# Strassen products in a hybrid decoder layer: seven half-size products for eight, hidden activations in DRAM, and a recurrence on doubling blocks

## The chip, the cores and the metric

The kernel runs on one core of a Trainium2 chip. A core has a matrix engine (TensorE, "PE" in the profile, with "PEld" for its weight loads), VectorE ("DVE"), ScalarE ("ACT"), GpSimd ("POOL") and SyncE ("SP"), which here issues all DMA transfers. Each runs its own list of instructions in order, and semaphores join them. The metric is the device time of one execution in microseconds.

## The reference

One decoder layer on 1024 tokens of width 1024, in float32, and a final norm.

```python
x = x + 0.5 * swiglu(rms(x), ffn1_w1, ffn1_w3, ffn1_w2)         # 1024 -> 2816 -> 1024
proj = rms(x) @ w_in                # q, f, i, og (8 heads x 128 each), pool 512, gates A and B
f = lb + (1 - lb) * sigmoid(f_r); k = 1 - f; q = silu(q_r); v = i_r
S_t = diag(f_t) S_{t-1} + k_t outer v_t;  o_t = S_t^T q_t       # per head, 128 x 128 state
y_a = (rms_per_head(o) * silu(og)) @ w_branch_a
y_b = (group_map(trailing_means(pool) - pool) * scale) @ w_branch_b
x = x + (sigmoid(ga) * y_a + sigmoid(gb) * y_b) @ w_out
x = x + 0.5 * swiglu(rms(x), ffn2_w1, ffn2_w3, ffn2_w2)
x = x + sigmoid(rms(x) @ ple_w_gate) * rms(p @ ple_w_proj)
return rms(x)
```

## The kernel before, in words

Every large product runs as three passes of float32r matmuls. `split` (L104 to L106) cuts a float32 operand into a high part (a ScalarE cast, L105) and a low part (a VectorE subtraction, L106); `mm3` (L119 to L122) sums high x high, high x low and low x high in PSUM. A full matmul has 128 x 128 stationary values and 512 moving columns.

There are two forms of product. `up` (L124) holds 128 weight columns stationary and moves 512 tokens: the result is feature-major, [128 features, 512 tokens], one PSUM bank, 8 chunks of the inner dimension, 24 matmuls. The token-major products (`down_tiles` L216, `down_half` L706 hold 128 tokens stationary and move 512 columns of weights. The residual `x` is token-major in SBUF as 16 tiles of [128, 512]; `norm_t` (L175) scales its rows, transposes them on TensorE against an identity (L187) and splits them into feature-major tiles.

`ffn` (L202) takes 22 chunks of 128 hidden features in groups of two. Of each chunk `up_chunk` makes w1 and w3 products for both halves of the tokens, the sigmoid gate and the split; `down_tiles` adds the chunk pair's part of the downward product to `x` at once (L224). The downward products run one group behind, and the hidden activations never leave SBUF.

In the mixing stage, `head_in` makes q, f, k and silu(og) of one head and half the tokens with `up`; v is made token-major for two heads at a time with 256 moving columns. `hgrn` (L417) runs the recurrence of one head over half the tokens in four chunks of 128: the decay between two tokens is a product of f's over blocks, in three steps of four neighbouring blocks (h = 1, 4, 16; score matmuls at L498 with 192 columns, or with ones at L505 and L506 where h = 1), and a last step between blocks of 64 tokens (L518). Masked copies (L510) put a step's scores in place, `grow` (L443) widens the blocks. Then follow k transposed (L531), the states of the chunks (L535, L544), the outputs (L553, L555), a norm per head and a transpose (L570). The heads' loop runs two inputs ahead. The gates, branch B, branch A, `w_out`, the second FFN and the embedding gate follow; the embedding's own product was made at the start and waits in DRAM.

The order of instructions on each engine is not written out. A planner goes through the program with a model of costs: program order gives the priority, an instruction may go ahead of an earlier one that isn't ready, and a tile's slot must be free before it is written. Tiles of one tag share a fixed number of slots: 54 units of [128, 512] ("u"), 12 split weight tiles of [128, 1024] ("w"), 4 raw weight tiles and some smaller sets. All DMA transfers go through SP's queue in planned order.

Of the kernel before, what the change touches and what calls it, by code (L numbers as in the profile page):

```python
# [15 lines left out]
AX = mybir.AxisListType  # L16
# [6 lines left out]
FC = 22  # L23
HEADS = 8
# [3 lines left out]
STEPS = (1, 4, 16)  # L28

N_RAW = 4  # L30
WARM = 11
N_W = 12
# units [128, 512]: main, temporaries, per chain of the recurrence (two tags each), states
BANKS = {"mm": 2, "aux0": 1, "aux1": 1, "sc0": 1, "sc1": 1}
UNITS = {"u": 54, "t": 4, "h0": 2, "h1": 2, "st": 3, "qx0": 1, "qx1": 1}
# [3 lines left out]
def hybrid_block(ctx: ExitStack, tc: tile.TileContext, a: dict, out: bass.AP):  # L39
    """One decoder layer and the final norm.  # L40

    Products run as three float32r passes: each float32 operand is split exactly into
    two parts of 12 bits (hi = round(x), lo = x - hi), and hi*hi + hi*lo + lo*hi is summed
    in PSUM.  The residual is held token-major; activations that feed a product with
    stationary weights are held feature-major, as hi and lo units [128, 512 tokens].
    """
    nc = tc.nc
    const = ctx.enter_context(tc.tile_pool(name="const", bufs=1))
    big = ctx.enter_context(tc.tile_pool(name="big", bufs=1))
# [9 lines left out]
    def unit(s, dt=F32, tag="u"):  # L59
        return big.tile([P, HALF], dt, tag=tag, name=name(s), bufs=UNITS[tag])  # L60

    def raw(s, shape=(P, 1024)):
        return big.tile(list(shape), F32, tag="raw", name=name(s), bufs=N_RAW)

    def wtile(s):
        return big.tile([P, 1024], F32R, tag="w", name=name(s), bufs=N_W)

    def bank(s="mm"):
        return psum.tile([P, HALF], F32, tag=s, name=name(s), bufs=BANKS[s])

# [4 lines left out]
    ident = small("ident", [P, P])  # L75
    make_identity(nc, ident)
    ones = small("ones", [P, P], F32R)
    nc.vector.tensor_scalar(ones, ident, 0.0, 1.0, ALU.mult, ALU.add)
# [3 lines left out]
    for h in STEPS:  # L82
        # columns of a step (see hgrn), rows s: 1 where s lies in the block of h tokens
        # that the column's target block takes as its source
        n = 32 // h
        m = small(f"mask{h}", [P, 192], BF16)
        nc.gpsimd.memset(m, 1.0)
        for at, blocks, first, move in ((0, 3, 0, 1), (96, 2, 0, 0), (160, 1, 1, 0)):
            mv = m[:, at : at + 32 * blocks].rearrange("p (a j h) -> p a j h", a=n, h=h)
            for sign, base in ((1, -first * h), (-1, first * h + h - 1)):  # L90
                nc.gpsimd.affine_select(
                    out=mv, in_=mv,
                    pattern=[[-sign * 4 * h, n], [-sign * move * h, blocks], [0, h]],
                    compare_op=ALU.is_ge, fill=0.0, base=base, channel_multiplier=sign,
                )
        masks[h] = m
# [11 lines left out]
    def load(ap, s):  # L108
        r = raw(s)
        nc.sync.dma_start(out=r, in_=ap)  # L110
        return r

    def weight(ap, s):
        r = load(ap, s)
        hi, lo = wtile(s + "h"), wtile(s + "l")
        split(r, hi, lo)
        return hi, lo

    def mm3(ps, ah, al, bh, bl, first, last):  # L119
        nc.tensor.matmul(ps, ah, bh, start=first, stop=False)  # L120
        nc.tensor.matmul(ps, ah, bl, start=False, stop=False)  # L121
        nc.tensor.matmul(ps, al, bh, start=False, stop=last)  # L122

    def up(w, act, half, off=0):  # L124
        """[128 columns, 512 tokens] of act @ w; w = (hi, lo) tiles whose column blocks of 128
        are the stationary operands."""
        ps = bank()
        n = len(act)
        for k in range(n):
            ah, al = act[k][half]  # L130
            c = slice(off + k * P, off + (k + 1) * P)
            mm3(ps, w[0][:, c], w[1][:, c], ah, al, k == 0, k == n - 1)
        return ps

    def token(act, k, t):
        ah, al = act[k][t // 4]
        c = slice((t % 4) * P, (t % 4 + 1) * P)
        return ah[:, c], al[:, c]

    def pair(s, tags=("u", "u")):  # L140
        return unit(s + "h", F32R, tags[0]), unit(s + "l", F32R, tags[1])

# [1 line left out]
    def rstd_of(rs, ss, n):  # L144
        nc.vector.tensor_tensor(rs, ss[:, 0:1], ss[:, 1:2], ALU.add)
        nc.vector.tensor_scalar(rs, rs, 1.0 / n, EPS, ALU.mult, ALU.add)
        nc.gpsimd.tensor_tensor(rs, rs, mhalf[:, 0:1], ALU.pow)  # L147
# [3 lines left out]
    def stat():  # L151
        stat_n[0] += 1
        ss = const.tile([P, 2], F32, tag="ss", name=name("ss"), bufs=4)
        rs = const.tile([P, 1], F32, tag="rs", name=name("rs"), bufs=4)
        return ss, rs

    def gain_rows(ap, s):
        g = raw(s)
        nc.sync.dma_start(out=g, in_=ap.partition_broadcast(P))
        return g  # L160

    def normed_row(x, g, t):
        """rms-normed token tile: two units [128 tokens, 512]."""
        ss, rs = stat()
        xn = [unit("xn"), unit("xn")]
        for d in range(2):
            nc.scalar.activation(xn[d], x[t][d], AF.Square, accum_out=ss[:, d : d + 1])
        rstd_of(rs, ss, D)
        for d in range(2):
            nc.vector.scalar_tensor_tensor(  # L170
                xn[d], x[t][d], rs[:, 0:1], g[:, d * HALF : (d + 1) * HALF], ALU.mult, ALU.mult
            )
        return xn

    def norm_t(x, g, between=None):  # L175
        """rms-normed x, feature-major and split: act[k][half] = (hi, lo).  Traces the first
        half of the tokens and returns a function that traces the second."""
        act = [[None, None] for _ in range(KC)]

        def rows(half):  # L180
            return [normed_row(x, g, 4 * half + t) for t in range(4)]

        def part(half, xn):
            for k in range(KC):
                ps = bank(("sc0", "sc1", "aux0", "aux1")[k % (2 + 2 * half)])
                for t in range(4):
                    nc.tensor.transpose(  # L187
                        ps[:, t * P : (t + 1) * P],
                        xn[t][k // 4][:, (k % 4) * P : (k % 4 + 1) * P],
                        ident,  # L190
                    )
                act[k][half] = pair("h")
                split(ps, *act[k][half])

        xn = rows(0)
        if between is not None:
            between()
        part(0, xn)
        return act, lambda: part(1, rows(1))
# [135 lines left out]
    def opening():  # L335
        for d in range(2):
            embed(0, d)
# [540 lines left out]
```

## Time and profile before

| | |
|---|---|
| timed runs | median 2550.24 us of 3 (2549.74 to 2550.61) |
| profiled execution | span 2549.6 us from first to last instruction; no other time of it is recorded, so the span stands 0.6 us under the median of the runs |
| PE busy | 2521.0 us, 11923 matmuls |
| weight loads | 2094.3 us |
| VectorE | 1227.1 us, 2132 instructions |
| ScalarE | 624.2 us, 1155 instructions |
| GpSimd | 57.7 us, 155 instructions |
| DMA | 154.19 MB, 60 GB/s over the span |
| granted TensorE clock | 0.999 |

Busy time adds up the durations of instructions. Matmuls are pipelined: one is listed with 0.39 us, but the next starts after about 0.23, so time per matmul is read from start times. A float32 matmul (not float32r) is listed as two records. "Idle before" is time in which an engine had nothing to run, with what ended it. A row of a group gives line, engine, operation, output and inputs by name, shapes and count, then busy time, mean nanoseconds of one, and the idle time before.

### The profile page before, as it was taken

The page shows a single profiled execution, that of the slowest core. Times are in us where ns is not written, and L with a number is a line of the kernel's source. Part 1 is how long each engine was busy: PE and PEld are TensorE (multiplying, and loading weights), DVE is VectorE, ACT ScalarE, POOL GpSimd, SP SyncE. Part 2 cuts the span into 40 slices and gives each one's busy share as a digit, 9 for nine tenths or more (in the row PEclk, how much of TensorE's full clock was granted, in tenths as well). Part 3 has the DMA queues.
Part 4 walks back from the last instruction along what each step waited for, and adds up shares of the span by engine and source line. Part 5 has one row for each costly group of instructions (what it writes and reads, how often), then busy time and mean ns, then how long its engine had stood idle before and what let it go on. Part 6 is the DMA issues. An engine that isn't in the chain of part 4 may idle for free.

```text
span 2549.6 us, 28969 instructions
## 1 busy us (share of the span) xinstructions
PE 2521.0 (99%) x11923; PEld 2094.3 (82%) x11923; DVE 1227.1 (48%) x2132; ACT 624.2 (24%) x1155; POOL 57.7 (2%) x155
## 2 busy tenths in 40 slices
PE   8999999999999999999999999999999999999998
PEld 6888888888888888888888888888888888888877
DVE  5344433333456758585852206344344334434475
ACT  6211111111124323333323113123111111111253
POOL 2000000000000000000000000000000000000010
PEclk9999999999999999999999999999999999999999
DMA  7111111111121111111111104321111111111132
GB/s 248 42 50 50 50 50 50 50 50 50 58 94 56 58 38 46 41 43 46 34 59 45 47 25 140 108 67 42 50 50 50 50 50 50 48 43 43 46 119 84
DMA packets 54372, 154.19 MB, mean 60 GB/s; under 512 B 6112, under 2 KB 6624, under 8 KB 54240
## 3 DMA queue, kind: packets, MB, share of 16 engines
q1 hardware_dynamic: 54240, 152.34, 18.4%
q8 instruction: 93, 1.52, 0.3%
q14 instruction: 39, 0.32, 0.0%
HBM read 135.54 MB, written 16.78 MB: 60 GB/s over the span
## 4 chain that ended last, share of the span: by engine, by line
PE 91%; DVE 5%; issue 1%; ACT 1%; DMA 1%; POOL 0%; SPq 0%; POOLq 0%; ACTq 0%; DVEq 0%
PE mm L121 22%; PE mm L122 22%; PE mm L120 22%; PE aux L120 6%; PE aux L121 6%; PE aux L122 6%; PE sc L498 2%; DVE score L510 1%; PE sc L187 1%; DVE xn L170 1%; PE aux L535 1%; PE aux L553 1%; PE aux L555 0%; PE aux L518 0%; POOL rs L147 0%
## 5 line engine op out<-in xcount | busy, mean ns | idle before, releaser
L224 DVE SCALAR_TENSOR_TENSOR x<-aux,x 128x512 f32<-128x512 f32 x352 | 241.2, 690 | 191.8 <-PE aux L122 190.3
L120 PE MATMUL aux<-w2h,gh 128*128 128x512 f32 x704 | 276.4, 393 | 1.6 <-DVE x L224 1.5
L120 PE MATMUL mm<-hh,w1h 128*128 128x512 f32 x704 | 274.9, 390 | 1.0 <-ACT hh L105 1.0
L121 PE MATMUL mm<-hl,w1h 128*128 128x512 f32 x704 | 274.6, 390 | 0.0
L122 PE MATMUL mm<-hh,w1l 128*128 128x512 f32 x704 | 274.5, 390 | 0.0
L121 PE MATMUL aux<-w2l,gh 128*128 128x512 f32 x704 | 274.3, 390 | 0.0
L122 PE MATMUL aux<-w2h,gl 128*128 128x512 f32 x704 | 274.0, 389 | 0.0
L120 PE MATMUL mm<-hh,w3h 128*128 128x512 f32 x704 | 274.0, 389 | 0.0
L122 PE MATMUL mm<-hh,w3l 128*128 128x512 f32 x704 | 273.9, 389 | 0.0
L121 PE MATMUL mm<-hl,w3h 128*128 128x512 f32 x704 | 273.9, 389 | 0.0
L211 DVE TENSOR_TENSOR sg<-sg,mm 128x512 f32<-128x512 f32 x88 | 60.5, 688 | 284.5 <-PE mm L122 284.5
L120 PEld LDWEIGHTS aux<-w2h,gh 128*128 128x128 f32 x704 | 132.1, 188 | 35.1 <-DVE x L224 8.3
L120 PEld LDWEIGHTS mm<-hh,w1h 128*128 128x128 f32 x704 | 132.1, 188 | 28.5 <-ACT hh L105 1.5
L122 PEld LDWEIGHTS aux<-w2h,gl 128*128 128x128 f32 x704 | 132.2, 188 | 27.8
L120 PEld LDWEIGHTS mm<-hh,w3h 128*128 128x128 f32 x704 | 132.2, 188 | 27.6 <-DVE x L746 0.2
L121 PEld LDWEIGHTS mm<-hl,w3h 128*128 128x128 f32 x704 | 132.2, 188 | 27.4
L122 PEld LDWEIGHTS mm<-hh,w3l 128*128 128x128 f32 x704 | 132.1, 188 | 27.4
L121 PEld LDWEIGHTS mm<-hl,w1h 128*128 128x128 f32 x704 | 132.2, 188 | 27.1
L122 PEld LDWEIGHTS mm<-hh,w1l 128*128 128x128 f32 x704 | 132.2, 188 | 27.0
L121 PEld LDWEIGHTS aux<-w2l,gh 128*128 128x128 f32 x704 | 132.2, 188 | 26.5
L120 PE MATMUL mm<-hh,wih 128*128 128x512 f32 x384 | 153.8, 401 | 0.0
L122 PE MATMUL mm<-hh,wil 128*128 128x512 f32 x384 | 153.5, 400 | 0.0
(234 smaller groups left out, 4286.0 us busy)
## 6 DMA issues: line engine op xcount, KB each, us to landing
w<-in_ffn_w_dram SPq DMA_DIRECT2D x132, 512.0 KB, 3.6
wi<-in_w_in_dram SPq DMA_DIRECT2D x24, 512.0 KB, 3.6
x<-in_x_dram SPq DMA_DIRECT2D x16, 256.0 KB, 7.4
e_dram<-e SPq DMA_DIRECT2D x16, 256.0 KB, 5.9
x_dram<-x SPq DMA_DIRECT2D x16, 256.0 KB, 2.0
wv<-in_w_v_dram SPq DMA_DIRECT2D x8, 512.0 KB, 3.5
o_dram<-og SPq DMA_DIRECT2D x16, 256.0 KB, 2.0
wgb<-in_w_in_dram SPq DMA_DIRECT2D x8, 512.0 KB, 3.5
```

The lines of the kernel that those rows point to most:

```text
L120: nc.tensor.matmul(ps, ah, bh, start=first, stop=False)
L121: nc.tensor.matmul(ps, ah, bl, start=False, stop=False)
L122: nc.tensor.matmul(ps, al, bh, start=False, stop=last)
L170: nc.vector.scalar_tensor_tensor(xn[d], x[t][d], rs[:, 0:1], g[:, d * HALF : (d + 1) * HALF], ALU.mult, ALU.mult)
L187: nc.tensor.transpose(ps[:, t * P : (t + 1) * P], xn[t][k // 4][:, (k % 4) * P : (k % 4 + 1) * P], ident,)
L211: nc.vector.tensor_tensor(s, s, pb, ALU.mult)
L224: nc.vector.scalar_tensor_tensor(x[t][d], ps, 0.5, x[t][d], ALU.mult, ALU.add)
L498: nc.tensor.matmul(ps[:, c, :192], kc[c], qx[:, c, :], start=True, stop=True)
L510: nc.vector.copy_predicated(s4[:, :, :, (4 - blocks) * hh :], sect(m4, lo, blocks), sect(ps, lo, blocks))
L535: nc.tensor.matmul(p_, a_, b_, start=True, stop=True)
L553: nc.tensor.matmul(p_, sc[:, c, :], vc[c], start=True, stop=s_ is None)
```

## The change

All large products but the embedding's use Strassen's scheme in Winograd's form: with each operand in four quarters, eight quarter products become seven products of sums and differences of quarters. The names are A for the weights' side (A11, A12, A22, S1 to S4) and B for the activations' side (B11, B21, B22, T1 to T3, N4); `SIDES` says which go together. The quarters are of the inner dimension (even and odd chunks of 128), of the weight columns (two chunks, such as w1 and w3 of one hidden chunk, or two column blocks of the projection) and of the tokens (two halves of 512).

- `prep` loads the two weight tiles of a pair, makes S1 to S4 with four GpSimd operations of [128, 512], and splits them: 10 tiles of the "w" tag, which has 12. `up_pair` runs seven products of 12 matmuls, and reads each result once with ScalarE or VectorE. `run_pair` leaves products 4 and 3 of a pair to run after products 1 and 2 of the next one.
- `act_first` makes B11 and B21 from the first half of the tokens after a norm; `act_second` makes the rest, with two VectorE differences from PSUM and two GpSimd differences for every two feature chunks. A full set takes 28 tiles of [128, 1024], all of tag "a".
- An FFN makes all 22 chunks first (`ffn_up`); the hidden activations and their sums (four GpSimd operations for two chunks) go to DRAM. `ffn_down` then reads them back in three groups of inner chunks (8, 8 and 6), with w2's quarters loaded and combined (six GpSimd differences of up to [128, 1024] a group, and two later), and x read again from DRAM.
- `tok` runs a token-major product: seven products, each over four blocks of 128 tokens, two lines of PSUM banks. After the fifth of the seven products (of the last group, in the downward one) the next norm's first half is begun.
- In the mixing stage v, the output gate, gates A and B, pooled and mixed values go through DRAM. v is made feature-major and transposed in `hgrn`. The loop over heads places one gate or pool pair behind each head. The recurrence takes seven levels (blocks of 1, 2, 4 to 64 tokens), each with four matmuls of 64 columns, a copy into the scores, and one multiplication that grows q's right halves and k's left halves together; before them, the diagonal comes from one product of k and q.
- Branch B's and A's activations are loaded and combined by `load_act`; `w_out` and the embedding gate combine both operands on GpSimd (`tok_sides`).
- silu is one ScalarE function instead of a sigmoid and a product. The host only moves axes (and repeats rows of w2 to fill its last group, which aren't used).

```diff
+ROOM = {"a": (1024, 28), "w": (1024, 12), "q": (1024, 4), "u": (512, 8), "h": (512, 5)}
+BANKS = {"pA": 2, "pB": 2, "pC": 1, "aux": 3}
...
+    def act_second(act, b11, b21, b12, b22):
+        t1, t3 = t_("w", "t1"), t_("w", "t3")
+        nc.vector.tensor_tensor(t1[:, L], b12, b11, ALU.subtract)
+        nc.vector.scalar_tensor_tensor(t3[:, L], b12, -1.0, b22, ALU.mult, ALU.add)
+        act["B22"].append(hilo_half(b22, "a", "x3"))
+        pool_sub(t1[:, R], b22, t1[:, L])
+        pool_sub(t3[:, R], b21, t1[:, R])
+        for t, names in ((t1, ("T1", "T2")), (t3, ("T3", "N4"))):
+            for n_, hl in zip(names, halves(hilo(t, "a", "x" + names[0]))):
+                act[n_].append(hl)
...
+        load(ra, wa)
+        load(rb, wb)
+        w = {}
+        w["A11"], w["A12"] = halves(hilo(ra, "w", "wa"), m)
+        pool_add(s[:, one], rb[:, one], rb[:, two])
+        pool_sub(s[:, two], s[:, one], ra[:, one])
+        w["S1"], w["S2"] = halves(hilo(s, "w", "ws"), m)
+        w["A22"] = hilo_half(rb[:, two], "w", "wd")
+        pool_sub(rb[:, one], ra[:, one], rb[:, one])
+        pool_sub(rb[:, two], ra[:, two], s[:, two])
+        w["S3"], w["S4"] = halves(hilo(rb, "w", "wt"), m)
...
+    SIDES = {
+        1: ("A11", "B11"), 2: ("A12", "B21"), 3: ("S4", "B22"), 4: ("A22", "N4"),
+        5: ("S1", "T1"), 6: ("S2", "T2"), 7: ("S3", "T3"),
+    }
...
+        pa, pb, pc = bank("pA"), bank("pB"), bank("pC")
+        product(1, pa, True)
+        nc.scalar.copy(c1, pa)
+        product(2, pc, True)
+        add(c1, c1, pc)
+        yield c1
+        product(6, pa, False)
+        nc.scalar.copy(c2, pa)
+        product(5, pb, True)
+        product(7, pa, False)
+        nc.scalar.copy(c3, pa)
+        add(c3, c3, pb)
+        yield c3
+        product(4, pa, False)
+        yield pa
+        product(3, pb, False)
+        add(c2, c2, pb)
+        yield c2
...
+        for i in order:
+            ls, rs = lhs(i), rhs(i)
+            line = int(i in (2, 5, 3))
+            start = i in (1, 2, 5)
+            for j in range(4):
+                if start:
+                    banks[line][j] = bank(TOK_TAGS[line][j])
+                ps = banks[line][j]
+                c = slice(j * P, (j + 1) * P)
+                for k, ((ah, al), (bh, bl)) in enumerate(zip(ls, rs)):
+                    mm3(ps, ah[:, c], al[:, c], bh, bl, start and k == 0, k == len(ls) - 1)
+                read(i, j, ps)
+            if i in between:
+                between[i]()
...
+        for hh in LEVELS:
+            n = 64 // hh
+            ps = bank("aux").rearrange("p (c x) -> p c x", c=4)
+            m = 64 if hh == 64 else P
+            for c in range(4):
+                right = qc[c].rearrange("p (a two h) -> p a two h", two=2, h=hh)[:, :, 1, :]
+                nc.tensor.matmul(ps[:m, c, :64], kc[c][:, :m], right, start=True, stop=True)
...
+            both = view(qk, hh, [[HALF - hh, 2], [2 * hh, na], [1, hh]])
+            by = view(tots[hh], 0, [[1, 2], [2, na], [0, hh]])
+            mul(both, both, by)
```

More of the change, by code (lines that the diff above doesn't have):

```diff
@@ L574, in hgrn @@
[L574 to L602 removed]
+        ps = bank("aux")
```

1191 lines of the change are left out of this document (609 added, 582 removed).

## The prediction

> **What bounds the kernel now.** I read the page's engine shares first, then its chain of waits, then busy time in stretches, then single instructions.
>
> ```profile
> span 2549.6 us, 28969 instructions
> PE 2521.0 (99%) x11923; PEld 2094.3 (82%) x11923; DVE 1227.1 (48%) x2132; ACT 624.2 (24%) x1155; POOL 57.7 (2%) x155
> PE 91%; DVE 5%; issue 1%; ACT 1%; DMA 1%; POOL 0%; SPq 0%; POOLq 0%; ACTq 0%; DVEq 0%
> ```
>
> In the table of stretches the columns are the stretch, its length, busy time and count of PE, weight loads, VectorE, ScalarE and GpSimd, the granted clock, the DMA share and GB/s.
>
> ```profile
> 100.00:700.00 600.00, 599.93 (x2643) 495.24 (x2642) 236.26 (x311) 99.39 (x130) 0.00 (x0) 1.00 0.15 49
> 740.00:1310.00 570.00, 560.94 (x3204) 480.40 (x3203) 406.90 (x950) 184.26 (x442) 17.95 (x19) 1.00 0.15 49
> 2540.00:2549.60 9.60, 1.76 (x15) 1.56 (x13) 3.59 (x9) 2.73 (x7) 0.55 (x1) 0.81 0.29 109
> ```
>
> TensorE is never without work: 28.6 us of the span are not PE, of which 8 lie at the end (2540 to 2549.6), 9 in the recurrence (740 to 1310) and the other 11 mostly at the start. In the first FFN (100 to 700) VectorE works 39% of the time and GpSimd not at all. So a matmul taken away is worth its whole pitch, as long as the other engines keep up. Pitch comes from start times, since a matmul's own 0.39 us overlaps the next:
>
> ```profile
> 863.79 0.39 PE L121 MATMUL mm<-hl,wih 128*128 128x512 f32 x1
> ...
> 866.51 0.39 PE L121 MATMUL mm<-hl,wih 128*128 128x512 f32 x1
> ...
> 900.66 0.28 PE L120 MATMUL mm<-wvh,hh 128*128 128x256 f32 x1
> ...
> 901.97 0.28 PE L122 MATMUL mm<-wvh,hl 128*128 128x256 f32 x1
> ```
>
> Twelve steps of 512 columns take 2.72 us, 0.2267 each; eleven of 256 columns take 1.31, 0.119 each.
>
> **The products.** Before, counted from the loops: each FFN 22 x 96 up and 22 x 48 down, 3168, so 6336; input projection 1152 (q, f, og), 192 (pool), 768 (gates); branch A 384, B 192, w_out 384, embedding gate 384: together 9792 of 512 columns, and 768 of 256 columns for v. That is 9792 x 0.2267 + 768 x 0.119 = 2311 us. After: 5544 in the FFNs (seven eighths), 26 pairs of projection columns at 84, 4 of branch B at 42, 4 of A at 84, 336 and 336: 8904, or 2019 us. **Minus 292 us.** The embedding product and the 256 norm transposes stay.
>
> **The recurrence on TensorE.** It runs 16 times (8 heads, 2 halves).
>
> ```profile
> 861.50 1.54 PE L498 MATMUL sc<-qx,k 128*128 128x192 f32 x8 [0.41 <-DVE score L510]
> 862.74 0.53 PE L120 MATMUL mm<-hh,wih 128*128 128x512 f32 x1
> ...
> 870.18 0.68 PE L518 MATMUL aux<-qf,k 128*64 128x64 f32 x8
> 870.79 0.50 PE L122 MATMUL mm<-hh,wil 128*128 128x512 f32 x1
> ...
> 881.38 0.34 PE L505 MATMUL sc<-qk,ones 128*128 128x384 f32 x1
> 881.56 0.34 PE L506 MATMUL sc<-qk,ones 128*128 128x384 f32 x1
> ...
> 898.02 0.60 PE L531 MATMUL aux<-ident,k 128*128 128x128 f32 x4
> 898.38 0.36 PE L120 MATMUL mm<-wvh,hh 128*128 128x256 f32 x1
> ...
> 899.30 1.16 PE L535 MATMUL aux<-v,k 128*128 128x128 f32 x8
> 900.22 0.36 PE L120 MATMUL mm<-wvh,hh 128*128 128x256 f32 x1
> ```
>
> Removed each time: two steps of four 192-column matmuls (1.24 each), four with ones at 0.18, two 512-wide ones (0.45) and the 64-token step (0.61): 4.3 us. Added: the diagonal (four 128-column ones, 0.92), four transposes of v (0.36), seven levels of four 64-column matmuls. Their price lies between 0.61 (64-wide weights) and 0.92 (128 columns) a level; most have full weights and half the columns, so I take 0.75: 5.25 in all. Net 2.2 x 16 = **plus 36 us** (20 to 55).
>
> **Can the other engines follow?**
>
> ```profile
> L106 DVE TENSOR_TENSOR w1l<-w,w1h 128x1024 fp32r<-128x1024 f32 x44 | 53.8, 1222 | 83.6 <-ACT w1h L105 83.5
> L105 ACT CAST w1h<-w 128x1024 fp32r<-128x1024 f32 x44 | 46.4, 1054 | 259.4 <-PE aux L121 172.7 <-issue 73.6 <-PE mm L121 10.8
> L224 DVE SCALAR_TENSOR_TENSOR x<-aux,x 128x512 f32<-128x512 f32 x352 | 241.2, 690 | 191.8 <-PE aux L122 190.3
> L167 ACT ACTIVATE xn<-x 128x512 f32<-128x512 f32 x64 | 39.8, 623 | 52.2 <-DVE x L224 33.4 <-DVE x L746 18.7
> L147 POOL TENSOR_TENSOR rs<-rs,mhalf 128x1 f32<-128x1 f32 x40 | 23.0, 579 | 1932.1 <-DVE rs L146 1870.5 <-DVE tot L440 48.2 <-DVE rs L145 5.3
> masks.py:199 POOL TENSOR_SCALAR_AFFINE_SELECT ident<-ident 128x128 f32<-128x128 f32 x1 | 0.3, 294 | 0.0
> L510 DVE COPY_PREDICATED score<-mask,sc 128x256 f32<-128x256 uint16 x48 | 25.6, 534 | 0.0
> L452 DVE TENSOR_TENSOR qf<-q,f 128x512 f32<-128x512 f32 x16 | 10.8, 677 | 0.0
> ```
>
> An upward pair is 84 matmuls, 19.0 us. VectorE has three 1024-wide splits and one 512-wide (4.4 us) and five 512-wide operations (3.4): 7.8 us. ScalarE has about 7. GpSimd, which did next to nothing, now makes the sums: four 512-wide ones a pair and four more every second pair. No two-input add of this size runs on it in the trace. From below an add costs VectorE's 0.68; from above, the pow row by its width is 579 ns per column, which would make the kernel impossible and is a power, not an add; nearest is the select, 294 ns for 128 columns, so 1.2 us for 512. Then GpSimd works 7 of 19 us. Twelve weight slots against ten used by a pair let the next two loads start after the second of seven products, about 13 us ahead of need; load, split and sums take about 7. So I cost the steady pairs at nothing; if that cover were gone, the load's 3.6 and the splits' 2.3 would come back at each of 70 pairs (410 us).
>
> A downward product is 48 matmuls, 10.9 us, with four 1024-wide splits and four reads: 7.7 us of VectorE. It follows, with less to spare.
>
> Beside these rows stands a rule of the Trainium skill (SBUF — State Buffer, "Who interferes with whom"): a GpSimd operation that reads SBUF and a VectorE operation with two SBUF inputs exclude each other for their whole length. No row here has both at work. By it the sum for an upward pair is unchanged, since 7 and 5 us still fit into 19; what it does at the downward groups is a rival below.
>
> **The new waits.** This decides. Before, the hidden activations stayed in SBUF and stages overlapped; now 28 wide slots are full of activation tiles during the upward products, so the next stage's tiles come from DRAM when those are let go.
>
> ```profile
> 30.00:40.00 10.00, 9.23 (x47) 7.31 (x46) 3.00 (x4) 5.82 (x10) 0.00 (x0) 1.00 1.02 363
> w<-in_ffn_w_dram SPq DMA_DIRECT2D x132, 512.0 KB, 3.6
> 20.19 0.69 PE L187 MATMUL sc<-ident,xn 128*128 128x128 f32 x2 [2.68 <-DVE xn L170]
> ...
> 20.82:23.54 2.72, 2.72 (x7) 2.14 (x7) 2.69 (x5) 0.42 (x1) 0.00 (x0) 0.50 0.61 209
> ```
>
> - **Up to down, twice.** Eight slots come free after product 2 of the last pair, seven products (19 us) before the array runs dry. In SP's queue stand eight w2 tiles, eight x tiles, then the first two chunk tiles: 18 x 0.524 = 9.4 MB. At 363 GB/s, the fastest stretch, that is 26 us; a third longer, 35. With 2.3 for the splits the wait is 9 to 18: 13 each, 26.
> - **Norm to up, twice.** Behind the last read: add 0.7, square 1.2, pow 0.6, scale 1.4, then four column groups at 4.4 us of VectorE (two PSUM reads, 2.5 widths of split), with copies and GpSimd's differences between them: about 25. Cover: products 1 and 2 (5.4), transposes (3), perhaps the next pair's first two. 12 each, 24; at the start 8.
> - **Embedding gate.** Its w tiles need slots that the FFN lets go at its end; 2.6 MB and splits, 12, and products 1, 2 wait for single-buffered splits, 4 each: 20.
> - **w_out.** 8 MB and the last y through DRAM; 15 with its own splits.
> - **Down groups.** Eight new w2 tiles at four changes of group, 4 each: 16.
> - **Branches B and A.** Half-size products (9.5 us a pair) with as many instructions, and A's last activations wait for B's: 18.
> - **Recurrence.** A level is a chain: four matmuls 0.75, masked copy 0.53, product of decays 0.68, handovers: 2.2 us, seven times 15, and some 17 around it (state, output, norm). 32 us a half, 64 a head, against some 58 us of matmuls for each odd head: 25.
>
> Sum of these, 152 (0 to 300). Nothing of it can be overtaken where tiles lack; below I keep zero because the order of instructions is planned and fills holes.
>
> **The clock.** After 2.68 us idle, matmuls ran at a granted clock of 0.50 for 2.72 us. About twelve of the waits are that long: 1.2 each, **14 us**. The Trainium skill (TensorE: Matmul & The Clock Gate, "What's actually happening") says the clock halves after an idle window of about 3.4 us; the trace halves after less. By the rule alone the gaps under its window would be free and this term about half.
>
> **The sum.** 2549.6 - 292 + 36 + 152 + 14 = 2460. The runs' median, 2550.24, is 0.6 above the span, so a timed run would read **about 2460 us**, 3.5% faster.
>
> **Rivals.**
> *The holes are filled.* For it: the planner kept the recurrence at 561 of 570 us on PE, though its chain runs over three engines. Against: a missing tile can't be planned around. Waits and clock together 50: 2549.6 - 256 + 50 = 2344 (2300 to 2390).
> *The port decides the downward groups.* Mechanism: at each group's start GpSimd makes six 1024-wide differences, 2.4 us each, 14.4, in which VectorE's splits can't run; in two products (21.7) VectorE needs 9.8 of splits and 5.5 of reads, together 29.7. Eight us late at six groups: 48, so 2508. That is the skill's exclusion named above; nothing here shows it yet.
> *Slower: the recurrence's chain ends last.* Place: one half can't begin its levels before the last has freed tiles (five narrow slots, four used by each). The stage holds 26 x 19.0 + 16 x 10 = 655 us of matmuls, 680 with my waits; the chain is 57 ahead plus 16 L. At L = 44.5 us a half it adds the 90 that make the whole gain vanish, so it decides there. At L = 50 it is 857, plus 177: 2637. For it: seven dependent levels where three wide steps stood, on a VectorE that is 71% busy in 740 to 1310. Against: ten gate and pool pairs of 19 us now lie between and behind the heads.
> That the matmuls don't fall in number would give some 2750; the seven calls leave no room for it.
>
> **How the numbers follow.** Forecast (2390 to 2540) 0.51; filled holes 0.24; port 0.07; chain 0.15; 0.03 for landing on the old time. A measurement of this kernel can tell about 0.2% (5 us). Faster 0.82, same 0.03, slower 0.15. The range 2330 to 2580 leaves out the lowest of the second case and most of the chain's.
>
> **What would show it.** Steady upward stretches with PE full and pairs every 19 us confirm the cover; PE gaps at the ends of the upward products ended by DMA, and at the norms by VectorE, confirm the waits. GpSimd's 512-wide adds at 1.2 us, VectorE's splits longer than 1.22 when they meet them: the port. Levels in the recurrence every 2.2 us and halves every 40 or less; over 44 the third rival holds. Wrong would be PE gaps inside steady pairs, or a matmul pitch off 0.227.

## The result, and the profile after

The changed kernel takes 2684.14 us (median; 2682.70 to 2688.28) where the kernel before, on the same chip, takes 2550.43: a ratio of 1.0525, 95% interval 1.051 to 1.054. It is slower by 134 us. The forecast was 2460, with 2330 to 2580 for the range.

From the page of the changed kernel: span, busy times, and DMA, which was 154.19 MB before.

```profile
span 2680.8 us, 29088 instructions
PE 2370.3 (88%) x10851; PEld 1920.4 (72%) x10851; DVE 1518.5 (57%) x1948; ACT 964.6 (36%) x1487; POOL 875.8 (33%) x674
DMA packets 117389, 299.98 MB, mean 112 GB/s; under 512 B 13312, under 2 KB 13824, under 8 KB 117248
```

TensorE was busy 2521 us of 2549.6 and is now busy 2370 us of 2680.8. So there are two findings: 282 us more in which it does nothing (310.5 against 28.6), and a busy time that fell by 151 us, where the prediction's matmuls account for 256 less (292 off, 36 on). No engine is full: it is a kernel of waits. The table of stretches says where they are. Its columns are those of the prediction.

```profile
150.00:200.00 50.00, 50.00 (x223) 41.39 (x222) 20.60 (x24) 16.65 (x24) 19.25 (x16) 1.00 0.34 105
1000.00:1050.00 50.00, 47.66 (x279) 39.23 (x279) 32.92 (x61) 16.08 (x32) 8.86 (x7) 1.00 0.24 83
1550.00:1600.00 50.00, 27.64 (x110) 19.59 (x109) 34.03 (x43) 17.59 (x26) 14.25 (x13) 0.84 0.87 294
1700.00:1750.00 50.00, 30.36 (x100) 22.07 (x99) 20.26 (x14) 6.08 (x6) 43.40 (x17) 0.73 0.44 161
2000.00:2050.00 50.00, 50.00 (x222) 41.42 (x221) 20.46 (x23) 17.06 (x25) 17.52 (x14) 1.00 0.30 94
```

Inside the upward products of both FFNs (150 and 2000) TensorE is full at the full clock; nothing was lost there. In the recurrence (1000) it misses 2.3 of 50 us. Between branches (1550) and in w_out (1700) it works 28 to 30 of 50 us, at a granted clock of 0.73 to 0.84. In w_out GpSimd is the busy one, 43 of 50 us.

The six longest waits stand at the joints between stages. In the timeline of TensorE, the bracket is the idle time ahead of the instruction and what ended it.

```profile
77.30 0.79 PE L148 MATMUL pA<-x0h,wah 128*128 128x512 f32 x1 [15.04 <-ACT wah L117]
...
522.11 0.79 PE L148 MATMUL pA<-w2h,gh 128*128 128x512 f32 x1 [22.02 <-ACT gh L117]
...
785.90 0.79 PE L148 MATMUL pA<-x0h,wah 128*128 128x512 f32 x1 [16.47 <-ACT wah L117]
...
1612.29 0.79 PE L148 MATMUL pA<-x0h,wah 128*128 128x512 f32 x1 [30.74 <-ACT wah L117]
...
1854.63 0.79 PE L148 MATMUL pA<-x0h,wah 128*128 128x512 f32 x1 [17.06 <-ACT wah L117]
...
2304.44 0.80 PE L148 MATMUL pA<-w2h,gh 128*128 128x512 f32 x1 [24.10 <-ACT gh L117]
```

They are the start, up to down (twice), norm to up (twice) and branch B to A: 125 us in six. Four end with `wah`, the high part of the *first weight* of a stage, and two with `gh`, a hidden tile. What held these back is read on the other engines.

**Norm to up.** In the timeline of SP's queue, the load of the projection's first weight:

```profile
759.87 0.38 SPq L140 DMA_DIRECT2D ra<-in_w_in_dram  x1
```

In ScalarE's, what it did up to this weight's split:

```profile
775.16 1.04 ACT L117 CAST xT1h<-t 128x1024 fp32r<-128x1024 f32 x1 [2.18 <-POOL t L90]
...
782.19 1.04 ACT L117 CAST xT1h<-t 128x1024 fp32r<-128x1024 f32 x1 [3.26 <-POOL t L90]
783.86 1.04 ACT L117 CAST xT3h<-t 128x1024 fp32r<-128x1024 f32 x1 [0.62 <-POOL t L90]
784.81 1.04 ACT L117 CAST wah<-ra 128x1024 fp32r<-128x1024 f32 x1
```

The weight's load was issued at 759.87, 25 us before its split at 784.81. ScalarE takes its instructions in planned order, in which the split of the weight stands behind every tile of `act_second`, and those wait for GpSimd's differences. Products 1 and 2 read only the first half's tiles, which had been ready.

**Up to down.** SP's queue at the end of the first FFN's upward products:

```profile
511.28 4.10 SPq L144 DMA_DIRECT2D gsS<-gs  x4
515.48 0.38 SPq L140 DMA_DIRECT2D x<-in_x_dram  x1
515.95 1.93 SPq L140 DMA_DIRECT2D gr<-gsA  x4
```

GpSimd's timeline in the same time:

```profile
503.82 2.34 POOL L90 TENSOR_TENSOR rB<-rB,t 128x1024 f32<-128x1024 f32 x1 [1.16 <-DVE w2l L118]
507.38 2.66 POOL L90 TENSOR_TENSOR rB<-rB,t 128x1024 f32<-128x1024 f32 x1 [1.22 <-issue]
510.00 1.25 POOL L87 TENSOR_TENSOR gs<-g,g 128x512 f32<-128x512 f32 x1
```

The loads `gr` of the first hidden tiles stand in SP's queue behind four stores `gsS`, which wait for GpSimd's last four sums (510.00 on), which stand in GpSimd's list behind the differences of w2. Products 1 and 2 of the first group read A11 and A12 of the first eight chunks, which had long been stored. It is a chain of queues: GpSimd, SP, then the loads and their splits.

**GpSimd and VectorE.** Groups of instructions, GpSimd's sums and one of VectorE's splits:

```profile
L87 POOL TENSOR_TENSOR s<-rb 128x512 f32<-128x512 f32 x74 | 98.6, 1333 | 582.4 <-PE pA L150 508.6 <-DMA rb<-in_w_in_dram 31.7 <-DMA rb<-in_ffn_w_dram 27.3
L118 DVE TENSOR_TENSOR w2l<-rB,w2h 128x1024 fp32r<-128x1024 f32 x50 | 74.3, 1504 | 12.5 <-ACT w2h L117 12.5
L90 POOL TENSOR_TENSOR rB<-rB,rB 128x1024 f32<-128x1024 f32 x18 | 52.0, 2889 | 1.1
```

A 512-wide sum takes 1.33 us on GpSimd (1.2 was forecast), a 1024-wide one where VectorE is at work 2.89. VectorE's split of 1024 takes 1.50 us beside it where the same form took 1.22 before.

**The ledger.** From all rows of TensorE's timeline, each matmul counted from its start to the next one's, less the idle time between, in us:

| | before | after | difference |
|---|---|---|---|
| products, 512 or 256 columns | 2372 | 2149 | -223 |
| norm transposes (256) | 27 | 55 | +28 |
| recurrence's matmuls (before, 32 of them are 512 wide) | 118 | 162 | +44 |
| idle between matmuls | 20 | 290 | +270 |
| behind the last matmul | 8 | 19 | +12 |
| first 11 warming ones | 5 | 5 | 0 |
| span | 2550 | 2681 | +131 |

At 0.2267 the products should have lost 292; most of the other 69 are steps at about twice that spacing (390 of 512 columns over 0.33 us, against 97). Of the 69, 54 lie where the granted clock was 0.50. Stretches of TensorE's idle time of 2 us or more number 27, where before there was one.

### The profile page after: what moved, and what is told of

Same layout as the page of the kernel before. It is cut to its first block, busy times and chain, and to the rows that moved or that the text cites. A ratio compares the mean times of both kernels' runs of the same rounds, so it can differ in the third digit from the quotient of the medians.

```text
span 2680.8 us, 29088 instructions
## 1 busy us (share of the span) xinstructions
PE 2370.3 (88%) x10851; PEld 1920.4 (72%) x10851; DVE 1518.5 (57%) x1948; ACT 964.6 (36%) x1487; POOL 875.8 (33%) x674
## 5 line engine op out<-in xcount | busy, mean ns | idle before, releaser
L148 PE MATMUL pA<-x0h,wah 128*128 128x512 f32 x304 | 125.0, 411 | 81.8 <-ACT wah L117 81.8
L150 PE MATMUL pA<-x0h,wal 128*128 128x512 f32 x304 | 124.1, 408 | 11.1 <-DVE wal L118 11.1
L148 PE MATMUL pA<-xT3h,wd 128*128 128x512 f32 x304 | 121.5, 400 | 10.2 <-ACT o L282 8.9
L118 DVE TENSOR_TENSOR gl<-gr,gh 128x1024 fp32r<-128x1024 f32 x84 | 103.2, 1230 | 37.8 <-ACT gh L117 37.5
L149 PE MATMUL pA<-x0l,wah 128*128 128x512 f32 x304 | 123.3, 406 | 0.0
L148 PE MATMUL pA<-xT1h,wsh 128*128 128x512 f32 x304 | 120.1, 395 | 1.7 <-ACT wsh L117 1.7
L150 PE MATMUL pA<-xT3h,wd 128*128 128x512 f32 x304 | 120.7, 397 | 0.0
L149 PE MATMUL pA<-xT3l,wd 128*128 128x512 f32 x304 | 120.2, 395 | 0.0
L148 PE MATMUL pC<-x0h,wah 128*128 128x512 f32 x304 | 120.1, 395 | 0.0
L149 PE MATMUL pC<-x0l,wah 128*128 128x512 f32 x304 | 120.1, 395 | 0.0
L150 PE MATMUL pC<-x0h,wal 128*128 128x512 f32 x304 | 119.6, 393 | 0.0
```

What stands on the lines that cost most here:

```text
L118: nc.vector.tensor_tensor(lo, src, hi.bitcast(F32), ALU.subtract)
L148: nc.tensor.matmul(ps, ah, bh, start=first, stop=False, **kw)
L149: nc.tensor.matmul(ps, ah, bl, start=False, stop=False, **kw)
L150: nc.tensor.matmul(ps, al, bh, start=False, stop=last, **kw)
```

## Experiments

Experiments 1 to 4, 5 and 6, 7 to 9, and 10 ran on one chip each, and each ratio is to the kernel before on the same chip (2550.1 to 2551.1; so differences between groups are sure to about 1 us). The theory from the traces: the loss comes from where the sums run and from two orders, at the norms and at the hidden tiles, and not from the seven products as such. The rival: the staging itself, its DMA volume and its dependences.

**1. The sums on VectorE.**

```diff
     def pool_add(o, x, y):
-        nc.gpsimd.tensor_tensor(o, x, y, ALU.add)
+        nc.vector.tensor_tensor(o, x, y, ALU.add)
```
(and `pool_sub` alike)

> The changed kernel with every sum and difference that GpSimd makes (875.8 us busy) put on VectorE. Theory (GpSimd's two-input sums are slow, 1.3 us for 512 columns, and keep VectorE's two-input operations out while they run): a group of two feature chunks behind a norm falls from 7.35 us to about 5.8, the stretches in which TensorE waits for GpSimd alone (1704 to 1750, 2556 to 2600) shrink by some 15 us each, splits come back to 1.22 us; total 40 to 90 us faster than the changed kernel, 2600 to 2645. Rival (VectorE, 57% busy, is now the one that ends last in the downward products, where it is at 72%): the same or slower than 2684, with TensorE gaps inside the downward products.

2588.31 us, 1.0149 (1.0132 to 1.0166) of before: 96 us less than the changed kernel, the largest effect of any edit and more than I had expected.

The page's busy times with the sums on VectorE:

```profile
PE 2350.3 (91%) x10851; PEld 1916.4 (74%) x10851; DVE 1757.4 (68%) x2480; ACT 969.0 (37%) x1487; POOL 47.8 (2%) x142
```

Its groups, one of w2's splits and a sum:

```profile
L118 DVE TENSOR_TENSOR w2l<-rB,w2h 128x1024 fp32r<-128x1024 f32 x50 | 60.2, 1219 | 10.4 <-ACT w2h L117 10.0
L87 DVE TENSOR_TENSOR s<-rb 128x512 f32<-128x512 f32 x74 | 50.8, 687 | 4.3 <-PE pA L150 3.8
```

VectorE makes the sums in 0.69 us and its splits are back at 1.22. 828 us of GpSimd's work became 239 more on VectorE, whose own splits had got shorter. TensorE's idle time between matmuls falls from 290 to 215: by about 20 at the changes from up to down, 18 at the embedding gate, 16 in w_out, 15 in the recurrence and 10 at the norms. At the branches it stays at about 52, and the wait of 30.74 is now 30.40, so GpSimd isn't what held those. The rival's sign, waits inside the downward products, shows in two of 4.6 us. An engine that was idle before the change was not free to use.

**2. Products 1 and 2 ahead of the second half's tiles.**

```diff
+        while hooks:
+            hooks.pop(0)()
...
-    second()
+    hooks.append(second)
```
(the first two lines stand in `run_pair` between product 2 and product 6; likewise for the norms ahead of the projection and of the second FFN)

> The changed kernel with one move: the second half of the tokens behind a norm is transposed, combined and split only after products 1 and 2 of the next stage's first pair, at the start, before the mixing stage and before the second FFN. Theory (those two products need nothing of the second half, but their weights' split stands behind all of it in ScalarE's and VectorE's lists): the gaps of 15.0, 16.5 and 17.1 us before the first product shrink to what remains behind 5.4 us of work, and the clock stays up: 15 to 30 us faster, 2655 to 2670. Rival (the second half's chain ends last anyway, so products only move): same within 5 us, 2680 to 2688.

2661.01, 1.0435 (1.0420 to 1.0451): 23 us less. The three waits of 15, 16 and 17 us are gone, but they left pieces of one to three us, here at the start, in TensorE's timeline of this kernel:

```profile
64.52 0.79 PE L148 MATMUL pA<-xT1h,wsh 128*128 128x512 f32 x1 [0.91 <-ACT xT1h L117]
...
73.08 0.80 PE L149 MATMUL pA<-xT1l,wsh 128*128 128x512 f32 x1 [3.19 <-DVE xT1l L118]
```

In the ledger idle time fell by 35 and the products rose by 14, 11 of them where the granted clock was 0.50: the products now run among the pieces, at the lower clock.

**3. The hidden tiles of products 1 and 2 ahead of w2.**

```diff
+            pre = {}
+            if x[0] is None:
+                for i in (1, 2):
+                    for q, m in zip(group, n):
+                        pre[i, q] = load(
+                            t_("a", "gr")[:, : m * HALF], gs[SIDES[i][0]][q][:, : m * HALF]
+                        )
             raws = [
```

> The changed kernel with one move: the four hidden tiles that the first two downward products read are loaded ahead of w2 and x. Theory (in SP's list their loads stand behind stores that wait for GpSimd's sums of the last chunks): the gaps of 22.0 and 24.1 us at the two changes from upward to downward shrink to 5 or less; 35 to 45 us faster, 2640 to 2650. Rival of the prediction (the transfers themselves, 9.4 MB, take the time): the w2 tiles are then late by as much, the gap stays over 12 us each, 2665 or more.

2658.07, 1.0423 (1.0407 to 1.0438): 26 us less, under what I expected. The first product begins 16 us sooner, and a second wait comes out behind it, in TensorE's timeline of this kernel:

```profile
505.93 0.80 PE L148 MATMUL pA<-w2h,gh 128*128 128x512 f32 x1 [6.16 <-ACT gh L117]
...
515.93 0.79 PE L150 MATMUL pA<-w2h,gl 128*128 128x512 f32 x1 [8.77 <-DVE gl L118]
```

VectorE's timeline ahead of the first `gl`:

```profile
502.59 11.08 DVE L118 TENSOR_TENSOR w2l<-rB,w2h 128x1024 fp32r<-128x1024 f32 x4
```

So about 13 of the 22 and 24 us were the place in SP's queue and not the 9.4 MB, which are still loaded. What is left hangs on VectorE's `gl`, which stands behind four splits of w2, 2.77 us each instead of 1.22 while GpSimd makes differences and sums.

**4. All three.**

> All three edits in one kernel. If they act at different places they add: 90 to 165 us faster than the changed kernel, 2520 to 2595. If VectorE becomes the bound instead: 2620 or more. With 2545 or less the changed scheme would beat the kernel before.

2555.49, 1.0024 (1.0014 to 1.0033): 129 us less, where the three alone sum to 145. That is nearly the whole loss, with the DMA volume unchanged (299.94 MB): the rival, the staging by itself, doesn't account for it. A version of the change stands level with the kernel before, and not ahead of it. The longest wait left in TensorE's timeline is the one between the branches:

```profile
1565.89 0.79 PE L148 MATMUL pA<-x0h,wah 128*128 128x512 f32 x1 [29.51 <-ACT wah L117]
```

A stretch of this kernel inside that wait, with the columns of the stretches above:

```profile
1536.40:1566.00 29.60, 0.11 (x1) 0.11 (x1) 27.09 (x34) 14.17 (x17) 0.00 (x0) 0.55 0.58 214
```

VectorE works 27.1 of 29.6 us there, on branch A's tiles, the first of which it makes as B's last product ends.

**5. The recurrence alone.** In the kernel before, the three steps and the last block are replaced by the seven levels:

```diff
-        for hh in STEPS:
-            qx = big.tile([P, 4, 192], F32, tag=f"qx{half}", name=name("qx"), bufs=1)
...
+        for hh in (1, 2, 4, 8, 16, 32, 64):
...
+            for c in range(4):
+                right = chunks(qf)[c].rearrange("p (a two h) -> p a two h", two=2, h=hh)[:, :, 1, :]
+                nc.tensor.matmul(ps[:m, c, :64], kc[c][:, :m], right, start=True, stop=True)
```

> The kernel before, with one part of the change alone: its recurrence goes through the seven levels of 1, 2, 4 to 64 tokens in place of three steps of four blocks and the last block; the products, their order and the SBUF tiles are those of the kernel before. Four 128-column matmuls give the diagonal, each level four 64-column matmuls. My theory: TensorE pays the levels at what the trace after showed, about 0.85 us each and some switching, so 16 halves cost 35 to 60 us more and the run takes 2585 to 2610. Rival: the recurrence's matmuls fit between others and the part costs nothing, 2545 to 2560; then all of TensorE's extra busy time in the changed kernel comes from its products and cold stretches. If the chain of seven levels ended last here, where no extra pairs stand between the heads, it would be over 2620.

2582.59, 1.0125 (1.0109 to 1.0141): plus 31.5 us, just under what I expected from the trace after, and near the prediction's plus 36. The page:

```profile
PE 2559.4 (99%) x12467; PEld 2132.7 (83%) x12467; DVE 1137.2 (44%) x1908; ACT 586.9 (23%) x1075; POOL 48.3 (2%) x149
```

TensorE is 99% busy, so the price is TensorE's own: 31.5 / 16 = 2.0 us a half. The products of experiment 4 or 9 with the recurrence of before were not run.

**6. The same order at the branches.** On top of experiment 4, the first half's tiles of a branch are built first, the rest behind products 1 and 2, and the last pair ahead of a branch isn't finished first.

```diff
         for i in range(len(src) // 2):
...
+            for n_, hl in zip(("B11", "B21"), halves(hilo(quarter(i, 0), "a", "x0"))):
                 act_[n_].append(hl)
-            act_second(act_, b1[:, L], b1[:, R], b2[:, L], b2[:, R])
+        hooks.append(go)
```
(`quarter` loads one half of the tokens; `go` loads both and calls `act_second`)

> The kernel of all three edits (sums on VectorE, first products ahead of the second half's tiles, hidden tiles ahead of w2), with the same order at the two branches: the first half's tiles of the pooled and of the recurrent branch are built first, the other five kinds of tile behind products 1 and 2 of the first pair (the first half is loaded a second time for that), and the last pair ahead of each branch is no longer finished before the next branch begins. Theory that the 29.5 us between branch B and A, and some 12 before B, stand for the order alone: 25 to 40 us less than 2555, so 2515 to 2530, below the kernel before. Rival: VectorE, which is 72 to 88% busy there with the sums, ends last whatever the order; then less than 12 us come off, 2543 to 2556.

2571.13, 1.0078 (1.0065 to 1.0091): 16 us *more* than experiment 4, outside both expectations. A stretch of experiment 6, with the columns of the stretches above:

```profile
1550.00:1600.00 50.00, 29.86 (x82) 19.84 (x83) 39.66 (x51) 19.93 (x24) 0.00 (x0) 0.63 0.48 162
```

The same stretch of experiment 4:

```profile
1550.00:1600.00 50.00, 34.11 (x141) 27.63 (x142) 43.48 (x55) 20.41 (x25) 0.00 (x0) 0.80 0.43 146
```

82 matmuls take 30 us, at a clock of 0.63. In the ledger idle time is the same (181 against 180) and the products take 11 us longer. The wait of 29.5 became 10.4, 9.2 and three of 2.6, ended by splits: the tiles' preparation ends last there whatever the order, which is the rival's reason though not its number, and matmuls strewn among the pieces run at the lower clock. (Loading the first half twice adds DMA too; it wasn't separated.)

**7. Matmuls of zeros in the holes**, on experiment 4: some 72 us of them ahead of the products that wait.

```diff
+    def idle(ps, n, start=False):
+        z, one = ident[:64, 64:].bitcast(BF16), ident[:64, :].bitcast(BF16)
+        for _ in range(2 * n):
+            nc.tensor.matmul(ps[:, :256], z, one, start=start, stop=False, skip_group_check=True)
...
+                if j == 0 and i in cold:
+                    idle(ps, cold[i], start)
```
(`cold` says ahead of which products, and how many; in `run_pair` alike)

> The kernel of all three edits, with matmuls of zeros (added to a bank that is started or summed anyway) where TensorE waits: 20 of 512 columns ahead of products 1 and 2 of each downward product's first group, 8 ahead of the first pair at each norm and 6 between the steps of its product 6, 60 ahead of branch A, 4 to 10 ahead of the first products of w_out and of the embedding gate; some 72 us of TensorE in 180 us of holes. Theory that the half clock behind the holes (some 50 us of excess start spacing in the kernel of all three edits) lies on the path: 15 to 35 us less than 2555, so 2520 to 2540, and the granted clock over 0.97. Rival: behind most holes VectorE sets the pace, so a faster clock only waits longer: the clock rises as much, the time by less than 8 us, 2547 to 2563.

2564.53, 1.0049 (1.0036 to 1.0061): 9 us more than experiment 4, just above what the rival gave.

The mean granted clock rose from 0.956 to 0.970, the products took 14 us less and idle time fell by 49, but 71 us of zeros came on. The run doesn't support the theory that the half clock can be bought back in this way; it doesn't show what the half clock costs by itself, since too many or ill-placed zeros hide a gain.

**8. Eight products in w_out and the embedding gate**, on experiment 4: no sums of quarters there, fewer splits, 96 matmuls (22 us) more.

```diff
-    tok((1, 2, 6, 5, 7, 3, 4), *tok_sides(b, raws), read)
+    for _ in tok8(b, raws, lambda t, d, ps: gate(t, d, ps, t_("u", "g"))):
+        pass
```
(`tok8` runs through the four quarters of the output, each with both quarters of tokens and of weights; w_out alike)

> The kernel of all three edits, with w_out and the embedding gate in eight half-size products again: no sums of quarters, 20 wide splits each instead of 28, but 384 matmuls instead of 336. Theory that VectorE ends last in these two: it loses some 18 sums and 8 splits of 1.22 us in each (30 us), TensorE gains 11 us in each; 10 to 35 us less than 2555, so 2520 to 2545. Rival, that the saved matmuls count there as everywhere: 22 us more, 2570 to 2580.

2558.95, 1.0027 (1.0017 to 1.0038), against 1.0024 for experiment 4: no difference. Neither expectation holds: the products take 16 us more, and about as much comes back: 9 of idle time, and the end behind the last matmul is 8.7 instead of 19.1 us. VectorE has 65 us less to do. In these two, seven products buy nothing.

**9. Eight products in the branches too**, on experiment 8: 72 more matmuls (16 us).

```diff
-        out_pair(a["w_branch_a"][j], a["w_branch_a"][j + 1], act, done)
+        out_pair8(a["w_branch_a"][j], a["w_branch_a"][j + 1], act, done)
```
(branch B alike; `out_pair8` runs one full product for each weight tile and each half of the tokens)

> The kernel before this one in the list (w_out and gate in eight products), with the two branches in eight products too: 48 matmuls a pair for B, 96 for A, 72 more in all (16 us), but no sums and no tiles of differences, so that VectorE has about 10 us for branch A's tiles where it had 30, and A's tiles fit beside B's. Theory that the branches' holes (some 60 us with those before and between) come from the preparation that seven products need: 25 to 45 us less than the kernel with eight products in w_out and gate alone, below 2510 if that one comes out at 2530. Rival: the 16 us of matmuls are added and the holes stay (B's start waits for the pool branch anyway): 5 to 20 us more than it.

2538.01, 0.9951 (0.9937 to 0.9964): 21 us less than experiment 8, a little short of the expected 25. **This is faster than both kernels**, by 0.5% and by 5.4%; 0.5% is small, but the runs don't overlap (2535.4 to 2540.8, the kernel before 2549.1 to 2551.9). The page's busy times:

```profile
PE 2383.2 (94%) x11019; PEld 1945.4 (77%) x11019; DVE 1622.5 (64%) x2300; ACT 914.1 (36%) x1407; POOL 48.5 (2%) x142
```

TensorE's timeline at the start of branch A:

```profile
1541.19 0.79 PE L148 MATMUL pA<-x0h,wah 128*128 128x512 f32 x1 [11.47 <-ACT wah L117]
```

With 16 us more of matmuls it is faster: idle time fell by 30, of which 17 at the wait between the branches (28.95 to 11.47). Only four pairs of products share a branch's tiles, and they didn't repay the making of them. Two things changed at once, fewer tiles for VectorE and room for A's tiles beside B's, and were not separated; nor were branch A and B.

**10. w2's differences later**, on experiment 9: taken ahead of product 6 instead of product 1.

```diff
+                if i == 6:
+                    differences()
```

> The kernel with eight products in both branches, w_out and gate, and w2's three differences T1, T2, T3 of a group taken just ahead of product 6, which is the first that reads one, instead of ahead of product 1. Theory that the two pieces of about 6 us at each change from up to down (the first ended by ScalarE's gh, the second by VectorE's gl) stand behind these six differences of 1.22 us on VectorE: 6 to 14 us less than 2538, so 2524 to 2532. Rival: the pieces are the loading of the four hidden tiles and the eight w2 tiles, and the differences come late for product 6 instead: within 4 us of 2538, or above.

2537.26, 0.9950 (0.9936 to 0.9963): as experiment 9. The rival's number, but not the rival's reason. VectorE's timeline of this kernel at the first change from up to down:

```profile
503.98 1.23 DVE L90 TENSOR_TENSOR t<-rB,rB 128x1024 f32<-128x1024 f32 x1
505.24 1.23 DVE L90 TENSOR_TENSOR rB<-rB,t 128x1024 f32<-128x1024 f32 x1
506.38 4.62 DVE L118 TENSOR_TENSOR gl<-gr,gh 128x1024 fp32r<-128x1024 f32 x4
```

The differences, written later, were still put ahead of the `gl` splits by the planner. The wait only changed its shape (2.4 and 11.1 us, where there were 6.2 and 6.6). What would bring `gl` forward stays open.

## Why the prediction was wrong, step by step

*Products, minus 292: right as a count and a pitch.* In the steady stretches 222 or 223 matmuls run in 50 us, as before. At full clock the saving is there; 69 us of it were eaten by slow steps, 54 of them at half clock, which belong to the clock below.

*Recurrence on TensorE, plus 36: right within 8.* In the changed kernel it takes 44 more than before in the ledger: a level takes 0.81 and not 0.75. Experiment 5 leaves out v's transposes (6.5 in the changed kernel); it shows 36 by the same count, of which 7 of idle time came back and the products took 3 more, so 31.5 of time.

*Steady upward pairs at nothing: right*, with GpSimd's sums at 1.33 instead of 1.2 us and TensorE full.

*New waits, 152: this step failed; with the end behind the last matmul they came to 282.* Idle time between matmuls by stage, in us, beside the forecast:

| stage | forecast | after |
|---|---|---|
| start, norm to up | 8 | 15 |
| up to down, twice | 26 | 48 |
| norm to up, twice | 24 | 55 |
| down groups | 16 | 6 |
| recurrence | 25 | 28 |
| branches | 18 | 52 |
| w_out | 15 | 34 |
| embedding gate | 20 | 36, and 12 more behind the last matmul |

The last column holds all idle time; before, all stages together had 20, 7 of them in the recurrence. The forecast named the places and mis-sized five of them by about two and the branches by nearly three, each by a reason that the runs show in part. For norm to up it took products 1 and 2 as cover; the first weight's split stood in ScalarE's list behind all that they should have covered (experiment 2 moved it). For up to down it added up DMA volume; a good half was the order of SP's queue behind GpSimd's late sums (experiment 3). For the branches it counted half-size products, not that A's tiles take VectorE some 30 us, which hardly begin before B ends (experiments 4, 6 and 9). For w_out and the gate it counted loads and splits; in the stretch at 1700 GpSimd's sums fill 43 of 50 us, and with the sums on VectorE about half of the idle time is gone at both. With all three edits 180 us of idle time are still there, so experiment 4 stands 95 us over the forecast.

*GpSimd's exclusion of VectorE* was a rival of 7%, priced at 48 us at the downward groups alone. Experiment 1 puts it and GpSimd's own slowness at 96 us. The place was wrong: at the groups only 6 us were lost, but the last hidden sums, the gate, w_out, the recurrence and the norms got shorter with it. Three causes in those 96 weren't separated: a sum that takes 1.33 us instead of 0.69, VectorE's work beside it stretched from 1.22 to 1.50, and a sum's place in GpSimd's list. How the two meet is seen where both have work back to back. Two 512-wide differences in GpSimd's timeline of the changed kernel, between the branches:

```profile
1583.01 3.26 POOL L90 TENSOR_TENSOR t<-b,t 128x512 f32<-128x512 f32 x2 [8.03 <-DVE t L182]
```

VectorE's timeline then:

```profile
1582.79 0.68 DVE L84 TENSOR_TENSOR o<-o,gb 128x512 f32<-128x512 f32 x1
1583.40 1.75 DVE L183 SCALAR_TENSOR_TENSOR t<-b 128x512 f32<-128x512 f32 x1
1585.07 1.75 DVE L118 TENSOR_TENSOR x<-b,x 128x512 fp32r<-128x512 f32 x1
```

The same split in the groups of the changed kernel:

```profile
L118 DVE TENSOR_TENSOR x<-b,x 128x512 fp32r<-128x512 f32 x18 | 24.6, 1365 | 0.0
```

In those of experiment 1, with GpSimd idle:

```profile
L118 DVE TENSOR_TENSOR x<-b,x 128x512 fp32r<-128x512 f32 x18 | 12.3, 685 | 0.0
```

The two take turns: GpSimd's 1.26 (near the 1.25 at 510.00 above), VectorE's 0.68, GpSimd's 1.26 again come to 3.20, against the 3.26 of the first row; and VectorE's 1.75 are about 1.1 of waiting and 0.68 of work. The Trainium skill (SBUF — State Buffer, "Who interferes with whom") says that such operations exclude each other for their whole length; these rows agree.

*The clock, 14: mis-sized too.* I took twelve waits at 1.2 us. There were 27 of 2 us or more and many shorter ones; slow products cost 69 us and the norm transposes 28, together 97. Not all of it need lie on the path (experiment 7 bought none of it back), but experiments 2 and 6 show products getting slower as waits are cut into pieces. A short wait is enough. TensorE's timeline of the changed kernel in a downward product:

```profile
603.86 0.65 PE L149 MATMUL pA<-w2l,gh 128*128 128x512 f32 x1 [1.77 <-DVE w2l L118]
```

The stretch behind it:

```profile
604.06:607.47 3.41, 3.41 (x9) 2.64 (x9) 3.41 (x4) 0.00 (x0) 1.31 (x1) 0.50 0.34 130
```

After 1.77 us idle the clock is at 0.50 for 3.4 us. By the Trainium skill's window of about 3.4 us (TensorE: Matmul & The Clock Gate, "What's actually happening"), which would have made the term smaller, this wait would be free; the clock of 0.50 behind it doesn't agree. A stretch of experiment 6:

```profile
1563.40:1594.10 30.70, 16.41 (x33) 9.64 (x34) 25.98 (x34) 12.94 (x15) 0.00 (x0) 0.50 0.54 177
```

It holds most of the wait of 9.2 us and the three of 2.6: the clock stays at half through all of them, with 3.3 us of matmuls between one and the next.

*Rivals.* The recurrence's chain as the end did not come: halves begin 32 us apart and levels 2.5, as the forecast had it (32 and 2.2).

```profile
1000.68 1.06 PE L673 MATMUL aux<-qk 128*128 128x128 f32 x8
1003.41 1.01 PE L700 MATMUL aux<-qk 128*128 128x64 f32 x8
1005.86 1.08 PE L700 MATMUL aux<-qk 128*128 128x64 f32 x8
...
1032.62 1.05 PE L673 MATMUL aux<-qk 128*128 128x128 f32 x8
```

That the planner fills the holes failed: at the norms and from up to down its order made a good part of them (experiments 2 and 3).

By the ledger, idle and the end behind it cost 282 instead of 152 (plus 130), slow steps some 97 instead of 14 (plus 83), and the recurrence 44 instead of 36 (plus 8): 2460 + 221 = 2681, the span.

## What to carry to other kernels

A product that is cheaper on TensorE is worth its matmuls only where the making of its operands is covered; cost that for each product separately, and keep the plain form where few products share the operands (here the two branches, four pairs each; in w_out and the gate it made no difference). At each joint write down the lists of every engine and queue in order and find what stands ahead of the first operand of the first product: at the norms and from up to down about half of the wait was a place in a list, and not a duration or bytes; between the branches it was VectorE's time. Work given to an idle engine is priced with what it does to its neighbours: a sum of 512 that takes 0.69 us on VectorE took 1.33 on GpSimd, one of 1024 up to 2.89 on the mean instead of 1.22, and both lengthened VectorE's own work.

## What was not expected of the hardware

A wait cut into pieces can cost more than the wait: with the same idle time (181 against 180 us), experiment 6 ran 11 us longer in its products, at a granted clock of 0.63 in the stretch. A wait of 1.77 us is enough for 3.4 us at half clock. Taking turns with GpSimd can double a short VectorE operation: 18 splits of 512 took 1.37 us on the mean instead of 0.69 (1.75 where one waits for the rest of a sum of 1.26), while w2's splits of 1024 took 1.50 instead of 1.22. Matmuls of zeros raised the granted clock from 0.956 to 0.970 and didn't shorten the run.
